# Forty of DOWN's 128 key blocks: both parts of the inputs in one matmul of 512 columns

## The chip, the cores and the metric

The kernel runs on one core of a Trainium2 chip. The metric is the device time of one execution in microseconds (us); the time before is the median of three runs. The engines are named as in the profile: PE is TensorE (PEld its weight loads), DVE is VectorE, ACT is ScalarE, POOL is GpSimd, and SP issues the DMAs of the weights.

## The reference

Two transformer blocks work one after the other on 256 tokens of width 1024, in float32. The change lies in the feed-forward layer of the first block, which picks experts by product keys. Cut to what matters:

```
qh = (xb @ w_pq).reshape(T, 8, 2, 128)                    # 8 heads, two half queries
s1, s2 = qh[:, :, 0] @ sub_keys1.T, qh[:, :, 1] @ sub_keys2.T
v1, i1 = top_k(s1, 16);  v2, i2 = top_k(s2, 16)           # routing, on VectorE here
cand_s = v1[..., :, None] + v2[..., None, :]              # 16 x 16 candidates
top_s, pos = top_k(cand_s, 16);  g = softmax(top_s)
a   = gelu(einsum(expert_down[eidx], xb))                 # DOWN
out = einsum(g * a, expert_up[eidx])                      # UP
```

The kernel gathers no experts. DOWN computes the products of all 16384 experts with all 256 tokens, takes the Gelu of them, and multiplies by a gate that is zero for experts that were not picked; UP sums over all experts.

## The kernel before

The expert matrix of DOWN is cut into 128 key blocks of 128 experts. Block j is one chunk `down{j}` of 128 x 1024 floats, that is eight weight tiles of 128 x 128. To be precise enough, each float32 operand is cut into a high and a low part: the chunk into `hi` and `lo`, the inputs into `XD[:, 0]` and `XD[:, 1]`. `unit_T` (line 343) makes three products for each of the eight tiles in `mm3` (lines 339 to 341): `hi` times the high inputs, `hi` times the low inputs, `lo` times the high inputs. All 24 matmuls of a block have 256 columns (the tokens) and add into one half of one PSUM bank; there are five such banks, tagged `mm`.

A chunk comes by DMA into `raw` (SP), is rounded into `hi` by ACT (line 123), and `lo = raw - hi` is made by POOL or by DVE (line 135). The table `PLAN` says which: POOL for blocks 0 to 20, DVE for 21 to 30, POOL for 31 to 47, and DVE from block 48 on. `Stream.take` runs ahead: when block j is taken, the program writes `hi` of block j+3 and `lo` of block j+2 into the engines' queues.

Each engine works through its own queue in the order in which the program wrote it. Behind the matmuls of block j, `ch.evac` first writes what reads the bank, `ev_down` (line 978; in DOWN's first blocks one Gelu on ACT from the bank to `cb[:, j]`, line 981), and then lets every running side chain take one step (`Chains.tick`). The side chain of importance here is `routing` (line 878). For each half of the tokens it takes 8 steps in which DVE searches the 16 best keys of two half heads (`top16`, lines 872 to 876, on 128 values), then 8 steps with the candidates of one head each (a sum in line 888 and `top16` on 256 values), then a softmax (lines 892 to 896, its exponential on ACT in line 893). Two ticks later PE transposes the result (line 899), and the gathering of the expert numbers follows (lines 902 to 926), with one more transpose on PE for each of the two key numbers (line 925). One step is written behind each block: the steps of the first 128 tokens behind blocks 0 to 15, their softmax behind block 16, the transpose behind block 18; for the second 128 tokens behind blocks 28 to 43, 44 and 46. When the routing is done the chain `gating` starts, which fills `cb` with gates while DOWN goes on.

Of the kernel before, what the change touches and what calls it, by code (L numbers as in the profile page):

```python
# [24 lines left out]
AF = mybir.ActivationFunctionType  # L25
OP = mybir.AluOpType
# [26 lines left out]
for _name, _w in (("avg", 3), ("aq", 4), ("mk", 2), ("mq", 2), ("mv", 4), ("mo", 4), ("xk", 8), ("xv", 8),  # L53
# [18 lines left out]
          ("keys", 0): 1, ("keys", 1): 1, ("keys", 2): 3, ("keys", 3): 1, ("keys", 4): 2, ("queries", 1): 3,  # L72
          ("gla", 1): 1, ("gla", 8): 1, ("gla_out", 2): 1}

PLAN = {"mv0": ("AV",), "xo2": ("AG",), "down21": ("AV",), "down31": ("AG",), "down48": ("AV",),
        "upw0": ("AV", "AG"), "upw122": ("AV",), "up3": ("AV", "AG"), "up31": ("AV",)}

# [72 lines left out]
class Chains:  # L150
# [23 lines left out]
    def evac(self, name, fns):  # L174

        self.held.append((name, fns))
        self.flush()
        self.tick()
# [30 lines left out]
def block_kernel(ctx, tc, xT, memT, pT, wst, dwn, upw, keysT, gate_w2, cols, rows, out):  # L209
    nc = tc.nc  # L210
    V, A, G, T = nc.vector, nc.scalar, nc.gpsimd, nc.tensor
# [17 lines left out]
    ws = Stream(nc, rawp, splitp, order, 3, 4)  # L229

    ws.plan = PLAN
    ch = Chains()
# [40 lines left out]
    def bank(pool, tag, **kw):  # L273
        return pool.tile([128, 512], FT, tag=tag, name=tag, bufs={"mm": 5, "at": 3}[tag], **kw)
# [63 lines left out]
    def mm3(ps, wh, wl, xh, xl, start, stop):  # L338
        T.matmul(ps, lhsT=wh, rhs=xh, start=start, stop=False)  # L339
        T.matmul(ps, lhsT=wh, rhs=xl, start=False, stop=False)  # L340
        T.matmul(ps, lhsT=wl, rhs=xh, start=False, stop=stop)  # L341

    def unit_T(pool, name, xs, evac, ks=range(8), needs=()):

        for c in needs:
            ch.finish(c)
        wh, wl = ws.take(name)
        ps = bank(pool, "mm")[:, :256]
        for i, kd in enumerate(ks):
            mm3(ps, wh[:, kd * 128:kd * 128 + 128], wl[:, kd * 128:kd * 128 + 128], xs[0][:, kd], xs[1][:, kd],  # L350
                i == 0, i == 7)
        ch.evac(name, [lambda: evac(ps)])

    def pair_T(pool, units, xs, at=6):
# [46 lines left out]
    with ExitStack() as es:  # L401
# [305 lines left out]
        def unit_first(name, i):  # L707
            key = f"{name}{i}"
            if name == "mv":
                unit_N(psA, [f"mv{k}" for k in range(4)], xs,  # L710
                       lambda tb, ps: A.activation(v1[:, tb, :, 0:128], ps.rearrange("p (h d) -> p h d", h=4), AF.Copy,
                                                   scale=rx[:, tb:tb + 1]))
            elif name == "mo":
                unit_N(psA, [f"mo{k}" for k in range(4)], xs, ev_mo)
            elif name == "avg":
                unit_N(psA, ["avg0", "avg1", "avg2"], xs, ev_avg, n=264)
            elif name == "aq":
                unit_T(psA, key, xs, times(aqT[:, i]))
            elif name in ("mk", "mq"):
                unit_T(psA, key, xs, lambda ps: ev_conv(ps, i + 2 * (name == "mk")))  # L720
            else:
                unit_T(psA, key, (memh, meml), split_times(kxh[:, i], kxl[:, i], Rm, G), needs=("mem",))
# [5 lines left out]
        for n in range(8):  # L728
            unit_T(psA, f"wo{n}", (mixh, mixl), add_and_prep(n, "g_cross", wk), ks=(4, 5, 6, 7, 0, 1, 2, 3),
                   needs=("window", "mlstm"))  # L730
# [65 lines left out]
    with ExitStack() as es:  # L796
        big = es.enter_context(tc.tile_pool(name="big", bufs=1))
        psD = psB = ctx.enter_context(tc.tile_pool(name="psD", bufs=4, space=PSUM))
        XD = big.tile([128, 2, 8, 256], FR)
        cb = big.tile([128, 128, 256], FT)  # L800
# [4 lines left out]
        J0 = 80  # L805
# [124 lines left out]
        front = {"j": 0, "t": 0}  # L930
# [16 lines left out]
        def gating():  # L947
# [10 lines left out]
            for t4 in range(64):  # L958
# [16 lines left out]
                    make(t4 // 2 * 8 + 8, t4 % 2)  # L975
                yield 1

        def ev_down(ps, j):
            t = front["t"]
            if t < 256:  # L980
                A.activation(cb[:, j, t:256], ps[:, t:256], AF.Gelu)
            if t > 0:
                A.activation(ps[:, 0:t], ps[:, 0:t], AF.Gelu)
                V.tensor_tensor(cb[:, j, 0:t], ps[:, 0:t], cb[:, j, 0:t], op=OP.mult)
            front["j"] = j + 1
# [7 lines left out]
        def coef(j):  # L993

            if j % 4 == 0:
                ring[0] = xp.tile([128, 4, 2, 256], FR, tag=("XH", "XL")[j // 4 % 2], name="ring")
            hi, lo = ring[0][:, j % 4, 0], ring[0][:, j % 4, 1]
            A.activation(hi, cb[:, j], AF.Copy, scale=1.0 / GATE)  # L998
            V.scalar_tensor_tensor(lo, cb[:, j], 1.0 / GATE, hi, op0=OP.mult, op1=OP.subtract)  # L999
            coefs[j] = hi, lo  # L1000

        for j in range(128):
            if j == 127:

                ch.finish("gating")
                coef(0)
                coef(1)
            unit_T(psD, f"down{j}", (XD[:, 0], XD[:, 1]), lambda ps, j=j: ev_down(ps, j), needs=("routing",) if j == J0 else ())

        sums = [[bank(psB, "mm") for tb in range(2)] for g in range(2)]  # L1010
        nat2 = flat[:, 4096:6144].rearrange("p (a d) -> p a d", a=2)
# [75 lines left out]
    with ExitStack() as es:  # L1087
# [409 lines left out]
        for n in range(8):  # L1497
            ps = bank(psA, "mm")[:, 0:256]
            for q4 in range(4):
                wh, wl = ws.take(f"dn{n * 4 + q4}")  # L1500
# [10 lines left out]
        for c in range(2):  # L1511
            wh, wl = ws.take(f"ple{c}")
            for i in range(4):
                ps = bank(psA, "mm")[:, 0:256]
# [123 lines left out]
```

## Time and profile before

| | us |
|---|---|
| median of 3 runs | 1550.6 (1550.4 to 1552.74) |
| the profiled execution, its own time | 1549.96 |
| its span, first to last instruction | 1548.3 |
| DOWN, first matmul | 283.6 |
| last matmul of DOWN | 686 |
| routing on VectorE, first 128 tokens | 282.9 to 335.7 |
| routing on VectorE, second 128 tokens | 367.7 to 418.7 |

The rows that the prediction reads stand in the section before it. All times of rows are microseconds from the start of the span. In a timeline a row has its start, its duration, the engine, the line, the operation and what it works on; matmuls overlap, so the pace of PE is read from the starts, not from the durations. On DVE and ACT too an instruction can start a little before the one ahead of it has ended, so what an instruction takes of its engine is read from start to start.

### The profile page before, as it was taken

How to read it: one execution, taken by the hardware profiler on the slowest of the kernel's cores; microseconds unless marked ns; L12 is line 12 of the kernel's file. 1: busy time of each engine (PE TensorE's matmuls, PEld its weight loads, DVE VectorE, ACT ScalarE, POOL GpSimd, SP SyncE). 2: the span in 40 equal slices, each digit the busy share in tenths (PEclk: the TensorE clock that was granted, in tenths of full speed). 3: DMA queues.
4: the chain of work that ended last, by engine and by line, in shares of the span. 5: the costliest groups of instructions: out<-in, count | busy, mean ns of one | idle time of the engine just before them, and what ended most of it. 6: DMA issues, size and time to landing. Idle time of an engine off the chain costs nothing.

```text
span 1548.3 us, 27502 instructions
## 1 busy us (share of the span) xinstructions
PE 1524.9 (98%) x10818; PEld 1417.4 (92%) x10818; DVE 1137.9 (73%) x2037; ACT 805.9 (52%) x1370; POOL 428.4 (28%) x239
## 2 busy tenths in 40 slices
PE   9899999999999999999999999998999999999998
PEld 8799999999999999998888888887888999999998
DVE  7977754877978899967777777768984656876456
ACT  7665553554545555454555445546754644544443
POOL 2220067654600000024444444403130000386000
PEclk9899999999999999999999999999999999999999
DMA  8335455456555554465666666655564465566553
GB/s 271 118 110 166 140 162 175 142 165 200 172 178 155 152 160 153 153 190 196 196 191 191 193 195 196 193 161 169 150 194 133 124 190 164 170 192 215 180 183 117
DMA packets 75713, 265.32 MB, mean 171 GB/s; under 512 B 8368, under 2 KB 11952, under 8 KB 75584
## 3 DMA queue, kind: packets, MB, share of 16 engines
q1 hardware_dynamic: 74848, 262.31, 54.0%
q8 instruction: 84, 1.38, 0.4%
q10 hardware_dynamic: 736, 1.27, 0.2%
q14 instruction: 45, 0.37, 0.1%
HBM read 262.49 MB, written 1.05 MB: 170 GB/s over the span
## 4 chain that ended last, share of the span: by engine, by line
PE 90%; DVE 6%; DMA 1%; ACT 1%; issue 1%; POOL 0%; SPq 0%; ACTq 0%; DVEq 0%; POOLq 0%
PE mm L339 18%; PE mm L341 18%; PE mm L340 18%; PE mm L1017 8%; PE mm L1018 8%; PE mm L1019 7%; PE mm L379 3%; PE mm L380 3%; PE mm L378 3%; PE at L964 2%; DVE lo L135 1%; DVE nww L298 1%; DMA rowt<-in_rows 0%; DMA memt<-in_memT 0%; DVE m L686 0%
## 5 line engine op out<-in xcount | busy, mean ns | idle before, releaser
L123 ACT CAST hi<-raw 128x1024 fp32r<-128x1024 f32 (+1 forms) x495 | 516.8, 1046 | 281.1 <-issue 169.0
L135 POOL TENSOR_TENSOR lo<-raw,hi 128x1024 fp32r<-128x1024 f32 x135 | 326.7, 2421 | 725.3 <-ACT hi L123 723.2
L135 DVE TENSOR_TENSOR lo<-raw,hi 128x1024 fp32r<-128x1024 f32 (+1 forms) x360 | 444.1, 1243 | 22.3 <-ACT hi L123 21.7
L339 PE MATMUL mm<-XD,hi 128*128 128x256 f32 x1024 | 295.6, 289 | 0.0
L340 PE MATMUL mm<-XD,hi 128*128 128x256 f32 x1024 | 289.7, 283 | 0.0
L341 PE MATMUL mm<-XD,lo 128*128 128x256 f32 x1024 | 289.5, 283 | 0.0
L999 DVE SCALAR_TENSOR_TENSOR ring<-cb,ring 128x256 fp32r<-128x256 f32 x128 | 172.6, 1350 | 92.5 <-ACT ring L998 92.5
L1017 PE MATMUL mm<-hi,ring 128*128 128x512 f32 x512 | 199.3, 389 | 0.0
L1018 PE MATMUL mm<-lo,ring 128*128 128x512 f32 x512 | 199.2, 389 | 0.0
L1019 PE MATMUL mm<-hi,ring 128*128 128x512 f32 x512 | 199.2, 389 | 0.0
L340 PEld LDWEIGHTS mm<-XD,hi 128*128 128x128 f32 x1024 | 196.2, 192 | 0.0
L341 PEld LDWEIGHTS mm<-XD,lo 128*128 128x128 f32 x1024 | 196.0, 191 | 0.0
L339 PEld LDWEIGHTS mm<-XD,hi 128*128 128x128 f32 x1024 | 196.0, 191 | 0.0
L339 PE MATMUL mm<-XH,hi 128*128 128x256 f32 x584 | 168.5, 289 | 1.5 <-DVE cb L390 0.9
L341 PE MATMUL mm<-XH,lo 128*128 128x256 f32 x584 | 165.9, 284 | 0.6 <-DVE lo L135 0.6
L340 PE MATMUL mm<-XL,hi 128*128 128x256 f32 x584 | 165.9, 284 | 0.0
L339 PEld LDWEIGHTS mm<-XH,hi 128*128 128x128 f32 x584 | 112.6, 193 | 3.1 <-issue 1.5
L1019 PEld LDWEIGHTS mm<-hi,ring 128*128 128x128 f32 x512 | 96.1, 188 | 20.1
L1017 PEld LDWEIGHTS mm<-hi,ring 128*128 128x128 f32 x512 | 96.1, 188 | 19.9
L1018 PEld LDWEIGHTS mm<-lo,ring 128*128 128x128 f32 x512 | 96.1, 188 | 19.7
L341 PEld LDWEIGHTS mm<-XH,lo 128*128 128x128 f32 x584 | 112.7, 193 | 0.8 <-DVE lo L135 0.8
L340 PEld LDWEIGHTS mm<-XL,hi 128*128 128x128 f32 x584 | 112.6, 193 | 0.2
(468 smaller groups left out, 2966.8 us busy)
## 6 DMA issues: line engine op xcount, KB each, us to landing
raw<-in_wst SPq DMA_DIRECT2D x237, 512.0 KB, 3.8
raw<-in_dwn SPq DMA_DIRECT2D x128, 512.0 KB, 3.7
raw<-in_upw SPq DMA_DIRECT2D x128, 512.0 KB, 3.9
hT<-in_xT SPq DMA_DIRECT2D x4, 256.0 KB, 4.7
memt<-in_memT SPq DMA_DIRECT2D x1, 1024.0 KB, 6.2
out<-hT SPq DMA_DIRECT2D x7, 128.0 KB, 1.7
rowt<-in_rows ACTq DMA_DIRECT2D x1, 640.0 KB, 6.7
raw<-in_wst SPq DMA_DIRECT2D x2, 256.0 KB, 3.6
```

Of the source, the lines that this page charges most:

```text
L123: self.nc.scalar.copy(hi[:, o], raw[:, o])
L135: (self.nc.vector if eng == "V" else self.nc.gpsimd).tensor_tensor(lo[:, o], raw[:, o], hi[:, o], op=OP.subtract)
L339: T.matmul(ps, lhsT=wh, rhs=xh, start=start, stop=False)
L340: T.matmul(ps, lhsT=wh, rhs=xl, start=False, stop=False)
L341: T.matmul(ps, lhsT=wl, rhs=xh, start=False, stop=stop)
L378: T.matmul(pss[tb], lhsT=xh, rhs=h, start=kd == 0, stop=False)
L379: T.matmul(pss[tb], lhsT=xh, rhs=l, start=False, stop=False)
L380: T.matmul(pss[tb], lhsT=xl, rhs=h, start=False, stop=kd == 7)
L999: V.scalar_tensor_tensor(lo, cb[:, j], 1.0 / GATE, hi, op0=OP.mult, op1=OP.subtract)
L1017: T.matmul(o, lhsT=ch, rhs=wh, start=j == 0, stop=False)
L1018: T.matmul(o, lhsT=ch, rhs=wl, start=False, stop=False)
L1019: T.matmul(o, lhsT=cl, rhs=wh, start=False, stop=j == 127)
```

## The change

For blocks 0 to 39 the block is computed by a new function, `unit_W`. It uses the whole bank: `hi` meets both parts of the inputs side by side in one matmul of 512 columns (the high inputs' sums in columns 0 to 255, the low inputs' in 256 to 511), and `lo` meets the high inputs in a matmul of 256 columns that adds into columns 0 to 255. That makes 16 matmuls in place of 24, with as many columns in all. The two sums of the bank are added on the way out by `ev_wide`: ACT copies columns 256 to 511 into `cb[:, j]`, DVE adds columns 0 to 255 to it, and ACT takes the Gelu of `cb[:, j]` in place. The Gelu of block j is written only with the evacuation of block j+1 (`settle`). Blocks 40 to 127 are as before.

```diff
+WIDE = 40
...
+    def unit_W(pool, name, x2, evac, needs=()):
...
+        for kd in range(8):
+            wide = lambda: T.matmul(ps, lhsT=wh[:, kd * 128:kd * 128 + 128], rhs=x2[:, :, kd], start=kd == 0,
+                                    stop=kd == 7)
+            if kd < 7:
+                wide()
+            T.matmul(ps[:, 0:256], lhsT=wl[:, kd * 128:kd * 128 + 128], rhs=x2[:, 0, kd], start=False, stop=False)
+            if kd == 7:
+                wide()
         ch.evac(name, [lambda: evac(ps)])
...
+        def settle():
+
+            if "open" in front:
+                j = front.pop("open")
+                A.activation(cb[:, j], cb[:, j], AF.Gelu)
+                front["j"] = j + 1
+
+        def ev_wide(ps, j):
+            assert front["t"] == 0
+            settle()
+            A.copy(cb[:, j], ps[:, 256:512])
+            V.tensor_tensor(cb[:, j], ps[:, 0:256], cb[:, j], op=OP.add)
+            front["open"] = j
+
         def ev_down(ps, j):
+            settle()
...
-            unit_T(psD, f"down{j}", (XD[:, 0], XD[:, 1]), lambda ps, j=j: ev_down(ps, j), needs=("routing",) if j == J0 else ())
+            needs = ("routing",) if j == J0 else ()
+            if j < WIDE:
+                unit_W(psD, f"down{j}", XD, lambda ps, j=j: ev_wide(ps, j), needs)
+            else:
+                unit_T(psD, f"down{j}", (XD[:, 0], XD[:, 1]), lambda ps, j=j: ev_down(ps, j), needs=needs)
```

Lines of the changed kernel are some 20 higher than those of the kernel before: 891 to 895 are the old 872 to 876 (`top16`), 907 is the old 888, 911 to 915 the old 892 to 896, 137 and 125 the old 135 and 123.

**VectorE at the start of DOWN.** Before, behind the last tile of `XD` only searches of the routing follow (`cb` is also the storage of the routing's tables):

```order
L866 TENSOR_TENSOR XD<-cb,XD 128x256 [waits Activation_49] x2
L872 MAX cb<-cb 128x8
L873 MAX_INDEX cb<-cb 128x8 [waits DVE_49]
L874 MATCH_REPLACE cb<-cb 128x128
L875 MAX cb<-cb 128x8 [waits DVE_49]
L876 MAX_INDEX cb<-cb 128x8 [waits DVE_49]
L872 MAX cb<-cb 128x8
```

With the change:

```order
L885 TENSOR_TENSOR XD<-cb,XD 128x256 [waits Activation_49] x2
L1008 TENSOR_TENSOR cb<-mm,cb 128x256 [waits Activation_49]
L891 MAX cb<-cb 128x8
L892 MAX_INDEX cb<-cb 128x8 [waits DVE_49]
L893 MATCH_REPLACE cb<-cb 128x128
L894 MAX cb<-cb 128x8 [waits DVE_49]
L895 MAX_INDEX cb<-cb 128x8 [waits DVE_49]
L891 MAX cb<-cb 128x8
```

The add of block 0 (line 1008) now stands ahead of the routing's first step, and the add of each further block up to 39 stands ahead of the step of that block.

**ScalarE at the same place.** Before, casts of the weights (`hi`) and Gelus from the bank (`mm`) take turns, and each Gelu waits only for PE:

```order
L123 CAST hi<-raw 128x1024 [waits DMAHW7_49,Pool_49]
L981 ACT_TABLE_LOAD
L981 ACTIVATE cb<-mm 128x256 [waits PE_49]
L123 CAST hi<-raw 128x1024 [waits DMAHW0_49,Pool_49]
L981 ACTIVATE cb<-mm 128x256 [waits PE_49]
L123 CAST hi<-raw 128x1024 [waits DMAHW1_49,Pool_49]
```

With the change:

```order
L125 CAST hi<-raw 128x1024 [waits DMAHW7_49,Pool_49]
L1007 COPY cb<-mm 128x256 [waits PE_49]
L125 CAST hi<-raw 128x1024 [waits DMAHW0_49,Pool_49]
L1001 ACT_TABLE_LOAD
L1001 ACTIVATE cb<-cb 128x256 [waits DVE_49]
L1007 COPY cb<-mm 128x256 [waits PE_49]
L125 CAST hi<-raw 128x1024 [waits DMAHW1_49,Pool_49]
L1001 ACTIVATE cb<-cb 128x256 [waits DVE_49]
L1007 COPY cb<-mm 128x256 [waits PE_49]
L125 CAST hi<-raw 128x1024 [waits DMAHW2_49,Pool_49]
```

Each Gelu now waits for DVE (its block's add), and the copy of the next block and the cast of a later chunk stand behind it.

**VectorE around the softmax of the first 128 tokens.** Before, the softmax, the reading of the transpose (`gT`), and the first steps of the gathering up to the first `lo` that DVE makes, that of block 21:

```order
L892 TENSOR_TENSOR cb<-cb 128x128
L894 TENSOR_REDUCE cb<-cb 128x8 [waits Activation_49]
L895 RECIPROCAL cb<-cb 128x8 [waits DVE_49]
L896 TENSOR_TENSOR cb<-cb 128x128 [waits DVE_49]
L902 TENSOR_SCALAR gT<-at 128x128 [waits PE_49]
L903 SCALAR_TENSOR_TENSOR gT<-at,gT 128x128 [waits DVE_49]
L907 TENSOR_SCALAR cb<-cb 128x128
L910 CAST cb<-cb 128x128 [waits DVE_49]
L912 CAST cb<-cb 128x256
L914 TENSOR_TENSOR cb<-cb,iota_96 128x2048 [waits DVE_49]
L135 TENSOR_TENSOR lo<-raw,hi 128x1024 [waits DMAHW1_49,Activation_49]
```

With the change:

```order
L911 TENSOR_TENSOR cb<-cb 128x128
L913 TENSOR_REDUCE cb<-cb 128x8 [waits Activation_49]
L914 RECIPROCAL cb<-cb 128x8 [waits DVE_49]
L915 TENSOR_TENSOR cb<-cb 128x128 [waits DVE_49]
L1008 TENSOR_TENSOR cb<-mm,cb 128x256 [waits Activation_49] x2
L921 TENSOR_SCALAR gT<-at 128x128 [waits PE_49]
L922 SCALAR_TENSOR_TENSOR gT<-at,gT 128x128 [waits DVE_49]
L926 TENSOR_SCALAR cb<-cb 128x128
L929 CAST cb<-cb 128x128 [waits DVE_49]
L931 CAST cb<-cb 128x256
L933 TENSOR_TENSOR cb<-cb,iota_96 128x2048 [waits DVE_49]
L137 TENSOR_TENSOR lo<-raw,hi 128x1024 [waits DMAHW1_49,Pool_49]
```

Between the softmax and the reading of the transpose stand the adds of blocks 17 and 18, which wait for copies on ACT; behind the shown rows come the add of block 19, the rest of the step and `lo` of block 22.

## Rows read from the trace of the kernel before

**Rows 1.** The page: busy time of each engine over the whole span, and the chain of work that ended last, by engine.

```profile
PE 1524.9 (98%) x10818; PEld 1417.4 (92%) x10818; DVE 1137.9 (73%) x2037; ACT 805.9 (52%) x1370; POOL 428.4 (28%) x239
...
PE 90%; DVE 6%; DMA 1%; ACT 1%; issue 1%; POOL 0%; SPq 0%; ACTq 0%; DVEq 0%; POOLq 0%
```

**Rows 2.** Busy time by stretch, four stretches of ten microseconds in which DOWN and the routing run together (start and end, length, busy time and number of instructions for each engine, granted clock as a share of 2.4 GHz, DMA share, GB/s).

```profile
core 0: us, PE busy (x) PEld busy (x) DVE busy (x) ACT busy (x) POOL busy (x), PEclk, DMA share, GB/s
...
300.00:310.00 10.00, 10.00 (x85) 10.00 (x85) 9.38 (x48) 4.20 (x7) 8.58 (x4) 1.00 0.61 183
...
320.00:330.00 10.00, 10.00 (x86) 10.00 (x85) 9.52 (x33) 4.05 (x7) 8.58 (x4) 1.00 0.61 179
380.00:390.00 10.00, 10.00 (x86) 10.00 (x85) 9.35 (x52) 4.47 (x7) 8.09 (x5) 1.00 0.54 168
400.00:410.00 10.00, 10.00 (x86) 10.00 (x85) 9.52 (x32) 4.64 (x7) 8.10 (x5) 1.00 0.56 178
```

**Rows 3.** Timeline of TensorE in DOWN (start in us, duration in us, engine, line, operation): a matmul of 256 columns, and the 24th one after it.

```profile
300.07 0.28 PE L341 MATMUL mm<-XD,lo 128*128 128x256 f32 x1
...
302.95 0.28 PE L341 MATMUL mm<-XD,lo 128*128 128x256 f32 x1
```

**Rows 4.** Timeline of TensorE in UP: a matmul of 512 columns, and the twelfth one after it.

```profile
850.12 0.39 PE L1019 MATMUL mm<-hi,ring 128*128 128x512 f32 x1
...
852.84 0.39 PE L1019 MATMUL mm<-hi,ring 128*128 128x512 f32 x1
```

**Rows 5.** Timeline of VectorE over the routing of the first 128 tokens: the first search of a first and of a second step (two half heads each), then the sums that open the first, the second and the last of the eight candidate steps, then the first subtraction of the softmax.

```profile
282.87 0.29 DVE L872 MAX8 cb<-cb 128x8 f32<-128x128 f32 x1
...
286.02 0.27 DVE L872 MAX8 cb<-cb 128x8 f32<-128x128 f32 x1
...
307.99 0.41 DVE L888 TENSOR_TENSOR cb<-cb 128x256 f32<-128x256 f32 x1
...
310.69 0.41 DVE L888 TENSOR_TENSOR cb<-cb 128x256 f32<-128x256 f32 x1
...
327.64 0.60 DVE L888 TENSOR_TENSOR cb<-cb 128x256 f32<-128x256 f32 x1
...
330.53 0.45 DVE L892 TENSOR_TENSOR cb<-cb 128x128 f32<-128x128 f32 x1
```

**Rows 6.** Timeline of VectorE just ahead of DOWN: a product of a PSUM bank with a tile, and the instruction behind it.

```profile
275.97 0.42 DVE L390 TENSOR_TENSOR cb<-mm,Rb 128x256 f32<-128x256 f32 x1 [2.46 <-PE mm L341]
276.31 0.89 DVE L862 SCALAR_TENSOR_TENSOR cb<-hT,colt,Rb 128x256 f32<-128x256 f32 x2
```

**Rows 7.** Timelines of ScalarE and of GpSimd in DOWN: the Gelu of a block, the cast behind it, and the subtraction on GpSimd that this cast lets start.

```profile
289.59 0.38 ACT L981 ACTIVATE cb<-mm 128x256 f32<-128x256 f32 x1 [1.56 <-PE mm L341]
289.87 1.04 ACT L123 CAST hi<-raw 128x1024 fp32r<-128x1024 f32 x1
...
290.98 2.43 POOL L135 TENSOR_TENSOR lo<-raw,hi 128x1024 fp32r<-128x1024 f32 x1 [0.47 <-ACT hi L123]
```

**Rows 8.** Timelines of TensorE, ScalarE and VectorE: DOWN's first matmul, then the softmax of the first 128 tokens and the transpose on TensorE that reads its last result (in brackets the idle time ahead, and who ended it).

```profile
283.56 0.36 PE L339 MATMUL mm<-XD,hi 128*128 128x256 f32 x1
...
334.48 0.31 ACT L893 ACTIVATE cb<-cb 128x128 f32<-128x128 f32 x1
...
334.83 0.29 DVE L894 TENSOR_REDUCE cb<-cb 128x8 f32<-128x128 f32 x1 [3.85 <-ACT cb L893]
...
335.39 0.29 DVE L896 TENSOR_TENSOR cb<-cb 128x128 f32<-128x128 f32 x1
...
338.35 0.27 PE L899 MATMUL at<-ident,cb 128*128 128x128 f32 x1
...
338.66 0.29 DVE L902 TENSOR_SCALAR gT<-at 128x128 f16<-128x128 f32 x1 [2.98 <-PE at L899]
```

**Rows 9.** Timelines behind that transpose: the cast and the table load on ScalarE, the subtractions of blocks 21 and 22 on VectorE, and the first matmul of block 21 on TensorE.

```profile
334.70 1.03 ACT L123 CAST hi<-raw 128x1024 fp32r<-128x1024 f32 x1
335.75 1.28 ACT L981 ACT_TABLE_LOAD   x1
...
340.92 1.22 DVE L135 TENSOR_TENSOR lo<-raw,hi 128x1024 fp32r<-128x1024 f32 x1
...
345.03 1.22 DVE L135 TENSOR_TENSOR lo<-raw,hi 128x1024 fp32r<-128x1024 f32 x1
...
344.22 0.28 PE L339 MATMUL mm<-XD,hi 128*128 128x256 f32 x1
```

**Rows 10.** Timelines over the routing of the second 128 tokens: the cast on VectorE that stands ahead of its first search, the last product of its softmax, the last matmul of block 46 and the transpose behind it.

```profile
367.68 0.29 DVE L926 CAST eT<-at 128x128 f16<-128x128 f32 x1 [3.29 <-PE at L925]
...
418.45 0.29 DVE L896 TENSOR_TENSOR cb<-cb 128x128 f32<-128x128 f32 x1
...
419.20 0.28 PE L341 MATMUL mm<-XD,lo 128*128 128x256 f32 x1
419.32 0.27 PE L899 MATMUL at<-ident,cb 128*128 128x128 f32 x1
```

**Rows 11.** Timelines of GpSimd and VectorE at one candidate sum, and the group of all 16 candidate sums (count, busy us, mean ns).

```profile
392.12 2.40 POOL L135 TENSOR_TENSOR lo<-raw,hi 128x1024 fp32r<-128x1024 f32 x1 [0.48 <-ACT hi L123]
...
393.02 1.78 DVE L888 TENSOR_TENSOR cb<-cb 128x256 f32<-128x256 f32 x1
...
L888 DVE TENSOR_TENSOR cb<-cb 128x256 f32<-128x256 f32 x16 | 10.1, 632 | 0.0
```

More of the change, by code (lines that the diff above doesn't have):

```diff
@@ L351, in unit_T @@
                 i == 0, i == 7)
+        ch.evac(name, [lambda: evac(ps)])
+    def unit_W(pool, name, x2, evac, needs=()):
+        for c in needs:
+            ch.finish(c)
+        wh, wl = ws.take(name)
+        ps = bank(pool, "mm")
+        for kd in range(8):
[6 more added lines that the diff above has]
+                wide()
         ch.evac(name, [lambda: evac(ps)])
```

## The prediction

> **What bounds the kernel now.** I read the page's busy times and the chain first: PE is busy for 98% of the span and makes 90% of the chain [rows 1]. That says that shorter PE work pays, but DVE's 73% is a mean over stages, so next I read the stretches in which DOWN and the routing overlap. There PE is busy without a gap at the granted clock 1.00, that is 2.4 GHz, ACT is half idle, and DVE is busy 9.35 to 9.52 of 10 us [rows 2]. The reader is to see that DVE is as full as PE there, and that this costs nothing today, because no matmul of blocks 0 to 20 waits for DVE: the banks are emptied by ACT, and POOL makes `lo`. Third, I read where PE and DVE meet. PE's transpose behind block 18 came 2.67 us after DVE's last softmax product had ended (335.68 against 338.35), and DVE then waited for PE [rows 8]. Behind block 46 the product ended at 418.74 and PE came at 419.32 [rows 10]: 0.58 us of room.
>
> **What PE saves.** 24 matmuls of 256 columns take 2.88 us [rows 3], 120 ns each. Twelve of 512 columns take 2.72 us [rows 4], 226.7 ns each. The columns stay the same and eight starts fall away: 8 x 226.7 + 8 x 120 = 2774 ns, which is 106 ns less than 2880. Over 40 blocks that is **4.25 us**, all of it on the path. No row shows a moving operand in two pieces 8 KB apart; bounds are 226.7 ns (UP's, one piece) and 240 ns (two of 256), the latter saving nothing. I take 226.7, since the columns of each piece lie together as UP's do.
>
> The Trainium skill (TensorE: Matmul & The Clock Gate, Back-to-back issue gap) puts a matmul's gap at its columns at 2.4 GHz plus some 2.5 ns, so eight starts would be 20 ns and 40 blocks 0.8 us. Here the fixed part is 120 - 106.7 = 13 ns in rows 3 and the same in rows 4, so the rows decide; by the page the forecast below would be 3.4 us later.
>
> **What DVE and ACT get.** DVE gets one add per block. Its nearest row, a product of a bank with a tile, lasts 0.42 us and the next instruction starts 0.34 later [rows 6]; I take 0.34, with 0.42 as the other end. ACT has a copy (0.28 from start to start, as the Gelu from a bank in rows 7) and a Gelu from SBUF (I take 0.3) in place of one Gelu: 0.3 us more per block of 2.77 on a half idle engine, hidden unless ACT is held. But it is held: in the new order each Gelu waits for DVE's add, and the next copy and the cast of a later chunk queue behind it. That cast (1.04) and POOL's `lo` (2.43) [rows 7] feed a block four further on, so some 6 us of lateness on DVE pass unseen, and more holds PE.
>
> **First hold-up, the softmax of the first 128 tokens.** A step of two half heads takes 286.02 - 282.87 = 3.15 us, the eight candidate steps with what precedes the softmax take 330.53 - 307.99 = 22.5 [rows 5]. With the add a step costs 3.49 and about 3.15 against PE's 2.774 per block, so DVE falls back at every block. Also, the routing now starts at 282.87, before DOWN's first matmul; then the add of block 0 stands ahead of it: 283.56 [rows 8] + 2.77 + 0.1 (drain) + 0.38 (copy) + 0.05 + 0.34 = 287.2, or 4.3 later. Sixteen more adds lie ahead of the softmax: 5.4. It starts at 330.53 + 4.3 + 5.4 = 340.2. Its wait of 3.85 for ACT disappears [rows 8], since ACT has by then done its copy; 0.45 + 0.31 (the exponential) + 0.85 (334.83 to 335.68) and hand-overs of 0.1 end it at 341.9. PE without a wait is through block 18 at 283.56 + 19 x 2.774 = 336.3. PE loses **5.6 us**, part of it already at blocks 14 to 18 by way of ACT's queue; the sum is the same.
>
> **Second, the change to DVE's `lo` at block 21.** Behind the exponential ACT has a cast (1.05 to the next start), a table load (1.29) [rows 9], the Gelu of 16, the copy of 17, a cast, the Gelu of 17 and the copy of 18 (0.3 + 0.28 + 0.94 + 0.3 + 0.38): 4.5 us. Only then can DVE add block 18, and in its queue the reading of the transpose stands behind that add: 4.9 us behind the exponential where PE's transpose would be ready at 1.25. So `lo` of block 21 comes 3.7 us later against PE. Today it ends at 342.14, 2.1 before the block's first matmul at 344.22 [rows 9], with the shorter blocks 1.9: 1.8 lost. `lo` of block 22 ends at 346.25 today, 0.85 ahead of that block (344.22 + 2.88); late by 3.7 and one more add, it costs another 1.7. The ends are 0 and 3.5; I take **3.0**, since ACT may make up a part while PE stands.
>
> **Third, the softmax of the second 128 tokens.** Its first step starts behind block 28 [rows 10], with 0.6 us more for the copy and add of that block, and 11 adds (blocks 29 to 39) make 3.7. PE comes 11 x 0.106 = 1.2 earlier, and the room is 0.58: 0.6 + 3.7 + 1.2 - 0.6 = **4.9 us**.
>
> **Fourth, the candidate sums.** They take 0.41 us alone [rows 5], 0.63 in the mean, and 1.78 where POOL was at work: that one ended 0.28 after POOL's instruction (392.12 + 2.40 = 394.52) [rows 11]. So it waited for POOL. Twelve of them will meet POOL at other phases: none waiting gives back 12 x 0.22 = 2.6; each waiting 1.37 costs 16.4 less that, 13.8. If DVE's add lets ACT go (0.3 + 0.28 + 1.04 + 0.1), POOL's `lo` ends 4.1 after the add, while the next sum would come after 3.15: that makes a step 3.6, 0.45 more. I count four such, **1.6 us** with rounding down, nearer to the mean row than to 1.78.
>
> Sum: -4.25 + 5.6 + 3.0 + 4.9 + 1.6 = **+10.9 us**. Against the profiled execution (1549.96, span 1548.3 and 1.7 around it) that is 1560.9; the median of the runs is 0.64 higher: **1561.5 us**. Nothing later gives it back, since PE is busy to the end; the one-block-late Gelu is settled at block 40, long before the gating reads it.
>
> **The rivals.** *DVE keeps up* (the adds hide in gaps): 1550.6 - 4.25 = 1546.3. For it speak ACT's idle half and the five banks; against it rows 2 and the arithmetic of 3.49 against 2.774 in one queue. 0.07. *One hold-up only*: DVE is late at the first softmax (5.6), but `lo` of 21 and 22 and the second softmax keep their room, because candidate sums that meet POOL less give up to 2.6 back: 1550.6 - 4.25 + 5.6 = 1552 less up to 2.6, no change. 0.08. *POOL decides*: the sums wait half of 13.8 instead of 1.6, which adds 5.3: 1567; it decides from the point where DVE's step, not PE's block, sets POOL's pace, and then each step is longer than the last sum assumes. 0.13. The Trainium skill (SBUF — State Buffer, Who interferes with whom) says that a DVE instruction with two SBUF inputs and a GpSimd one that reads SBUF exclude each other for the whole instruction; rows 11 agree, and the same page frees the new add, which has one SBUF input. *The wide matmul is paced as two of 256*: nothing saved, 1565.8 at most, less where DVE sets the pace anyway; 0.04. The TensorE page's smaller saving would land between that and the forecast and has no chance apart from it, as rows 3 and 4 measure the fixed part. That the change doesn't take place I leave out: the program has the 16 matmuls.
>
> **How the numbers follow.** My forecast, three hold-ups that outweigh the saving, has 0.68: 1561.5, from 1554.3 (no loss at block 21, sums that give 2.6 back) to about 1565. The rival on the other side, DVE keeping up, is the one below 1547.5. With POOL deciding and 0.08 per add in place of nothing (28 x 0.08 = 2.2) the upper end is 1569. Range 1554 to 1569. A measurement of this kernel tells some 0.2%, 3.1 us, from no change. Faster 0.07, same 0.08, slower 0.85.
>
> **What would show it.** The wide matmuls' starts alternate 227 and 120 ns. In the stretch 284 to 330 DVE has no idle time and each add comes later behind its block, up to some 8 us; ACT's Gelus wait for DVE. PE stands at the transpose behind block 18 and at the one behind block 46, several us each, with DVE's softmax product as the releaser, and at blocks 21 and 22 for `lo`. Blocks 23 to 39 run at 2.774. If PE has no wait at these places, the step that counted DVE's queue was wrong; if only the amounts differ, the meeting with POOL was.

## The result and the profile after

The changed kernel takes 1568.86 us (median of 4 runs, 1566.77 to 1570.41) against 1550.57 us before in the same job: the ratio is 1.0114, 95% interval 1.0101 to 1.0128. It is slower by 18.3 us, where 10.9 was forecast: the forecast is 7.4 us short, and the time lies 0.14 us below the upper end of its range. The profiled execution took 1570.41 us, its span 1568.5 us.

The page of the changed kernel, busy times and chain, answers to [rows 1]: PE has 320 matmuls fewer and 6 us more of busy time, and DVE's share of the chain rose from 6% to 14%.

```profile
PE 1530.6 (98%) x10498; PEld 1405.5 (90%) x10498; DVE 1156.0 (74%) x2077; ACT 818.8 (52%) x1410; POOL 428.1 (27%) x239
...
PE 82%; DVE 14%; ACT 1%; DMA 1%; issue 1%; POOL 0%; SPq 0%; ACTq 0%; DVEq 0%; POOLq 0%
```

DOWN, from its first to its last matmul, went from 402.76 us (283.56 to 686.32) to 419.85 us (286.14 to 705.99): 17.1 us of the difference lie there, where the change is. DOWN also starts 2.6 us later, in code that the change does not touch; the last two experiments below are about that.

**The saving.** TensorE's timeline in DOWN, answering to [rows 3]: a wide matmul and, sixteen starts on, the same one of the next block.

```profile
300.68 0.40 PE L364 MATMUL mm<-XD,hi 128*128 128x512 f32 x1
300.91 0.28 PE L368 MATMUL mm<-XD,lo 128*128 128x256 f32 x1
301.03 0.40 PE L364 MATMUL mm<-XD,hi 128*128 128x512 f32 x1
...
303.50 0.39 PE L364 MATMUL mm<-XD,hi 128*128 128x512 f32 x1
```

The starts alternate 0.23 and 0.12 us, and a block takes 303.50 - 300.68 = 2.82 us, not 2.774. With 120 ns for the narrow one, a wide matmul takes 2820 / 8 - 120 = 233 ns, between the bounds of 226.7 and 240, and 40 blocks save 2.4 us, not 4.25.

**DVE falls back.** VectorE's timeline: the add of block 0 and the first search, the add of block 8 with the first candidate sum behind it, a later sum, and the softmax.

```profile
289.65 0.42 DVE L1008 TENSOR_TENSOR cb<-mm,cb 128x256 f32<-128x256 f32 x1 [4.13 <-ACT cb L1007]
290.00 0.28 DVE L891 MAX8 cb<-cb 128x8 f32<-128x128 f32 x1
...
317.44 0.40 DVE L1008 TENSOR_TENSOR cb<-mm,cb 128x256 f32<-128x256 f32 x1
317.77 1.03 DVE L907 TENSOR_TENSOR cb<-cb 128x256 f32<-128x256 f32 x1
...
339.10 1.01 DVE L907 TENSOR_TENSOR cb<-cb 128x256 f32<-128x256 f32 x1
...
346.20 0.28 DVE L911 TENSOR_TENSOR cb<-cb 128x128 f32<-128x128 f32 x1
...
347.41 0.29 DVE L915 TENSOR_TENSOR cb<-cb 128x128 f32<-128x128 f32 x1
```

A step of two half heads takes (317.44 - 289.65) / 8 = 3.47 us with its add; 3.49 was forecast, from the 3.15 of [rows 5]. A candidate step takes (346.20 - 317.77) / 8 = 3.55 us; 3.15 was forecast. The row of GpSimd's timeline and the group of all candidate sums on VectorE (count, busy us, mean ns) answer to [rows 11]:

```profile
337.44 2.39 POOL L137 TENSOR_TENSOR lo<-raw,hi 128x1024 fp32r<-128x1024 f32 x1 [1.23 <-ACT hi L125]
```

```profile
L907 DVE TENSOR_TENSOR cb<-cb 128x256 f32<-128x256 f32 x16 | 16.1, 1008 | 0.0
```

The sum at 339.10 ended at 340.11, 0.28 behind POOL's instruction (339.83), and the mean sum takes 1008 ns in place of 632.

**PE stands.** TensorE's waits between 284 and 455 us (line, released by, us in total, times, longest). Before there is none in this stretch.

```profile
PE at L918 <- ACT hi L125: 11.0, 2, 5.8
PE mm L368 <- POOL lo L137: 1.7, 4, 0.6
PE mm L368 <- DVE lo L137: 0.9, 1, 0.9
PE mm L343 <- POOL lo L137: 0.7, 2, 0.5
```

The first row is the two transposes behind blocks 18 and 46. The profile names ACT's cast as their releaser. That cast ended at 347.76 (its row is below), DVE's last product at 347.41 + 0.29 = 347.70, and the weight load of the transpose began at 347.82. It was DVE's product that counted: in four traces PE waits at both transposes (this one, and those of the way out alone, of the stands filled and of POOL still, below), and in all eight waits the weight load begins 0.115 or 0.116 us behind the end of DVE's product, but anything from 0.059 to 0.065 behind the end of the cast. The cast ends just there because it too stood behind the exponential, which waited for DVE. The chain runs from add to search to sum on DVE without a break from 290 to 346.2. Timelines of ScalarE and TensorE there, the cast and the table load answering to [rows 9], the transpose to [rows 8]:

```profile
346.51 0.31 ACT L912 ACTIVATE cb<-cb 128x128 f32<-128x128 f32 x1 [1.70 <-DVE cb L911]
346.73 1.03 ACT L125 CAST hi<-raw 128x1024 fp32r<-128x1024 f32 x1
347.77 1.28 ACT L1001 ACT_TABLE_LOAD   x1
...
342.31 0.40 PE L364 MATMUL mm<-XD,hi 128*128 128x512 f32 x1
347.85 0.45 PE L918 MATMUL at<-ident,cb 128*128 128x128 f32 x1 [5.14 <-ACT hi L125]
```

**And then the clock falls.** Busy time by stretch around the two stands, in the columns of [rows 2]:

```profile
340.00:345.00 5.00, 2.71 (x15) 2.13 (x15) 4.76 (x17) 2.80 (x4) 2.38 (x1) 1.00 0.49 120
345.00:352.00 7.00, 4.15 (x14) 3.60 (x15) 3.31 (x12) 5.46 (x9) 2.37 (x1) 0.51 0.29 80
352.00:356.00 4.00, 4.00 (x24) 3.50 (x24) 3.97 (x8) 2.37 (x6) 0.00 (x0) 1.00 0.27 108
429.00:434.00 5.00, 2.77 (x24) 2.56 (x22) 4.76 (x17) 0.00 (x0) 1.53 (x1) 0.99 0.67 206
434.00:440.70 6.70, 3.11 (x15) 3.14 (x16) 6.00 (x19) 4.42 (x7) 0.00 (x0) 0.50 0.14 27
440.70:445.00 4.30, 4.30 (x38) 4.30 (x38) 4.16 (x7) 1.96 (x3) 0.00 (x0) 1.00 0.52 201
```

The reader is to see the column before the last but one: 1.00, then 0.51 and 0.50 (that is 1.2 GHz), then 1.00 again. In both places PE had stood and came back to work at the lower level. No stretch of DOWN in the kernel before shows that.

**The sum of DOWN**, from the starts of the blocks in TensorE's timelines, each against the same block before, less 0.06 us up to block 39:

| | forecast | measured |
|---|---|---|
| 40 shorter blocks | -4.25 | -2.4 |
| blocks 15 to 18, short waits and the first stand | 5.6 | 8.1 |
| block 19 at the lower clock | none | 1.8 |
| wait for `lo` of blocks 21 and 22 (measured: of 22 alone) | 3.0 | 1.1 |
| blocks 43, 44, 46, short waits and the second stand | 4.9 | 7.2 |
| block 47 at the lower clock | none | 1.3 |
| candidate sums | 1.6 | in the hold-ups |
| sum | 10.9 | 17.1 |

### The profile page after: what moved, and what is told of

The parts are those of the page before. It is cut to its first block, busy times and chain, and to the rows that moved or that the text cites. A ratio compares the mean times of both kernels' runs of the same rounds, so it can differ in the third digit from the quotient of the medians.

```text
span 1568.5 us, 26977 instructions
## 1 busy us (share of the span) xinstructions
PE 1530.6 (98%) x10498; PEld 1405.5 (90%) x10498; DVE 1156.0 (74%) x2077; ACT 818.8 (52%) x1410; POOL 428.1 (27%) x239
## 4 chain that ended last, share of the span: by engine, by line
PE 82%; DVE 14%; ACT 1%; DMA 1%; issue 1%; POOL 0%; SPq 0%; ACTq 0%; DVEq 0%; POOLq 0%
PE mm L341 15%; PE mm L343 15%; PE mm L342 15%; PE mm L1057 7%; PE mm L1055 7%; PE mm L1056 7%; PE mm L399 3%; PE mm L398 3%; PE mm L397 3%; PE at L983 2%; DVE lo L137 1%; DVE cb L895 1%; DVE cb L892 1%; DVE cb L894 1%; DVE cb L893 1%
## 5 line engine op out<-in xcount | busy, mean ns | idle before, releaser
L341 PE MATMUL mm<-XD,hi 128*128 128x256 f32 x704 | 205.4, 292 | 0.0
L343 PE MATMUL mm<-XD,lo 128*128 128x256 f32 x704 | 199.7, 284 | 0.7 <-POOL lo L137 0.7
L342 PE MATMUL mm<-XD,hi 128*128 128x256 f32 x704 | 199.7, 284 | 0.0
L343 PEld LDWEIGHTS mm<-XD,lo 128*128 128x128 f32 x704 | 135.5, 192 | 1.1 <-POOL lo L137 1.1
L342 PEld LDWEIGHTS mm<-XD,hi 128*128 128x128 f32 x704 | 135.8, 193 | 0.0
L341 PEld LDWEIGHTS mm<-XD,hi 128*128 128x128 f32 x704 | 135.6, 193 | 0.0
```

## The experiments

Theory Q: what is lost comes from DVE's queue, by the added adds and by the sums that meet POOL, and the lower clock follows from PE's stands. Rival M: the wide matmuls themselves make it. The first four kernels below were timed beside before at 1550.03 us; the one with the quiet blocks, the two with the inputs side by side and the one with the later transposes beside 1550.38; the others beside 1550.26. Lengths of DOWN are from first to last matmul, 402.76 before and 419.85 after.

**The way out alone.** Blocks 0 to 39 by narrow matmuls, with the changed way out:

```diff
-                unit_W(psD, f"down{j}", XD, lambda ps, j=j: ev_wide(ps, j), needs)
+                unit_T(psD, f"down{j}", (XD[:, 0], XD[:, 1]), lambda ps, j=j: ev_wide(ps, j), needs=needs)
...
-            A.copy(cb[:, j], ps[:, 256:512])
-            V.tensor_tensor(cb[:, j], ps[:, 0:256], cb[:, j], op=OP.add)
+            A.copy(cb[:, j], ps[:, 0:256])
+            V.tensor_tensor(cb[:, j], ps[:, 0:256], cb[:, j], op=OP.max)
```

> Blocks 0 to 39 are computed as in the kernel before (24 matmuls of 256 columns), but leave their bank in the changed way: a copy on ACT, an operation of the add's size on DVE (the larger of the copy and the bank, which are equal), the Gelu one block later. Theory Q (DVE's queue carries the loss): PE stands at the transposes behind blocks 18 and 46 as in the changed kernel, the granted clock falls to 0.50 behind each stand, and the time is 1569 to 1571 us: the 0.06 us that a wide block saves is lost too, but for the blocks whose lateness is hidden by the stands. Rival M (the wide matmuls themselves make the loss): no stand, 1550 to 1551 us.

Measured: 1568.63 us, ratio 1.0122 (1.0105 to 1.0139), DOWN 420.32 us. Its waits of TensorE in the same stretch:

```profile
PE at L918 <- ACT hi L125: 10.9, 2, 5.8
PE mm L343 <- POOL lo L137: 1.3, 4, 0.5
PE mm L343 <- DVE lo L137: 0.7, 1, 0.7
```

The stands are those of the changed kernel, with not one wide matmul in the program. Rival M falls. The time is 0.4 us below what was expected. The 2.4 us of the wide matmuls are worth only 420.32 - 419.85 = 0.5 us beside them: a PE that reaches the transpose earlier stands there longer.

**Without the add.**

```diff
-            A.copy(cb[:, j], ps[:, 256:512])
-            V.tensor_tensor(cb[:, j], ps[:, 0:256], cb[:, j], op=OP.add)
+            A.copy(cb[:, j], ps[:, 0:256])
```

> Wide matmuls in blocks 0 to 39, but DVE's add is left out: ACT copies columns 0 to 255 and takes the Gelu one block later, so the products of the low inputs are missing from the result. Theory Q: no stand at the transposes, clock 1.00 through all of DOWN, blocks of 2.82 us in place of 2.88, so 1550.6 - 40 x 0.06 = 1548.2 us. Rival A (ACT's doubled work and its order hold the casts): stands remain, over 1555 us. Rival M (wide matmuls): about 1568 us.

Measured: 1548.99 us, ratio 0.9994 (0.9984 to 1.0004), DOWN 400.20 us, 2.56 less than before. Busy time where the changed kernel stood:

```profile
340.00:345.00 5.00, 5.00 (x30) 4.39 (x29) 4.90 (x9) 3.56 (x8) 0.00 (x0) 1.00 0.48 121
345.00:352.00 7.00, 7.00 (x42) 6.11 (x41) 5.86 (x8) 4.08 (x8) 0.00 (x0) 1.00 0.59 216
```

PE is busy without a gap, at 2.4 GHz. The copy and the second Gelu on ACT are hidden. The whole difference of 419.85 - 400.20 = 19.65 us hangs on one DVE instruction per block, 0.33 us from its start to the next (317.44 to 317.77 above): on its own time, 40 x 0.33 = 13 us of DVE, and on ACT's wait for it, which goes with it here. An add that ACT doesn't wait for was not run; the run with POOL still, below, shows what the meeting of the sums with POOL is worth of it.

**The stands filled.** Forty matmuls that nobody needs, ahead of each of the two transposes:

```diff
-                ps = bank(psD, "at")[:, 0:128]
+                ps = bank(psD, "at")
+                for _ in range(40):
+                    T.matmul(ps[:, 0:256], lhsT=XD[:, 0, 0, 0:128], rhs=XD[:, 0, 0], start=True, stop=True)
+                ps = ps[:, 0:128]
                 T.transpose(ps, ee, ident)
```

> The changed kernel with 40 additional matmuls of 256 columns (4.8 us at 0.12) ahead of each of the two transposes that read a softmax, so that PE works through most of the time in which it stood; their result is not used. Theory Q with the clock: the granted clock stays 1.00 behind blocks 18 and 46, blocks 19 and 47 take 2.82 and 2.88 us in place of 4.72 and 4.28, and the time falls by 1.9 + 1.4 = 3.3 us to 1565.6 us though 80 matmuls were added. Rival (the clock falls there for another reason than PE's stand): both drops remain and the time is 1569 us or more.

Measured: 1565.95 us (1565.32 to 1566.88), ratio 1.0104 (1.0088 to 1.0121), DOWN 418.45 us. The same stretches:

```profile
345.00:352.00 7.00, 6.62 (x46) 5.98 (x46) 3.30 (x12) 5.26 (x10) 2.40 (x1) 1.00 0.20 73
352.00:356.00 4.00, 2.80 (x16) 2.14 (x15) 3.93 (x10) 2.26 (x5) 0.00 (x0) 1.00 0.35 123
...
434.00:440.70 6.70, 5.70 (x48) 5.52 (x48) 6.00 (x19) 4.14 (x7) 0.00 (x0) 1.00 0.10 18
```

Of its waits of TensorE between 284 and 455 us:

```profile
PE mm L368 <- DVE lo L137: 2.6, 2, 1.4
```

The clock stays at 1.00 in all of them: it had fallen because PE stood. But of the 3.3 us only 1.4 came back in DOWN, those of block 47 (the other 1.5 us by which the median fell lie outside DOWN, where nothing was changed). Behind the first stand the full clock brought PE sooner to blocks 21 and 22, and there it lost 4.26 + 4.45 - 2 x 2.82 = 3.1 us (lengths of the two blocks) to waits for `lo`, in place of 1.1. So the lower clock cost nothing of its own at the first stand; it lay on a wait that was there anyway. The time came out near the 1565.6 us expected, but not by that sum.

**POOL still during the sums.**

```diff
+NO_LO = {f"down{j}" for j in (*range(8, 21), *range(36, 48))}
...
             raw = self.raws.pop(c)
+            if self.order[c][0] in NO_LO:
+                self.parts[c] = (hi, hi)
+                self.second += 1
+                continue
```

> The changed kernel, but POOL makes no lo for blocks 8 to 20 and 36 to 47: their matmuls read hi twice, so the product with the low weights is wrong there. POOL is idle while DVE makes the candidate sums. Theory Q with the meeting of the sums and POOL as one of its terms: each sum takes 0.41 us in place of 1.01, DVE ends each softmax some 4.8 us earlier, the hold-ups of 8.2 and 7.2 us shrink to about 3.4 and 2.4, and the time is 1555 to 1559 us (the lower end if the clock no longer falls). Rival (the sums' waits lie in time in which DVE would have been idle): 1566 to 1569 us.

Measured: 1558.78 us, ratio 1.0055 (1.0038 to 1.0071), DOWN 409.89 us. The group of the candidate sums:

```profile
L912 DVE TENSOR_TENSOR cb<-cb 128x256 f32<-128x256 f32 x16 | 6.6, 414 | 0.0
```

DOWN is 9.96 us shorter than in the changed kernel, half of the 19.65. A sum takes 414 ns in place of 1008, 9.5 us less for sixteen, and the hold-ups shrink from 8.1 to 3.9 and from 7.2 to 1.9 us: together 9.5. From its first search DVE reaches the first softmax 4.2 us sooner, and its eight sums up to there are 4.2 us shorter. The Trainium skill (SBUF — State Buffer, Who interferes with whom) says that a DVE instruction with two SBUF inputs, which this sum is, and a GpSimd instruction that reads SBUF exclude each other; the 1008 and the 414 ns agree. The time is at the upper end of what was expected, since behind the first hold-up the clock fell again (block 19 took 5.27 us).

**Wide blocks only where DVE does not search.**

```diff
-WIDE = 40
+WIDE = {*range(17, 28), *range(47, 57)}
...
-            if j < WIDE:
+            if j in WIDE:
```

> Wide matmuls only in blocks 17 to 27 and 47 to 56, between the stretches in which DVE searches; the way out of these blocks is the changed one. Theory Q: DVE has room there, no stand over 1 us, clock 1.00 through DOWN, and 21 blocks save 0.06 us each: DOWN takes 401.6 us in place of 402.9, the time is about 1549 us, not to be told from before. Rival (the way out costs wherever it stands, by the order on ACT): stands at the transposes behind blocks 18 and 46 again, above 1555 us.

Measured: 1550.16 us, ratio 1.0004 (0.9995 to 1.0014), DOWN 402.94 us. No stand, as expected, but no gain either. TensorE's waits from 284 to 470 us, of which before has none:

```profile
PE mm L368 <- DVE lo L137: 0.6, 2, 0.4
PE at L983 <- DVE hots L964: 0.5, 1, 0.5
```

PE now waits for DVE's `lo` of blocks 22 and 27 and for the first operand of the gating behind block 57. These three blocks are longer by 0.4, 0.6 and 0.6 us, a little more than the wide matmuls save. That it is the 21 adds that make DVE late there is argued, not shown by a run of its own.

**High and low inputs side by side in memory**, once without the add and once in the quiet blocks:

```diff
-        XD = big.tile([128, 2, 8, 256], FR)
+        XK = big.tile([128, 8, 2, 256], FR)
+        XD = XK.rearrange("p n a t -> p a n t")
...
-            wide = lambda: T.matmul(ps, lhsT=wh[:, kd * 128:kd * 128 + 128], rhs=x2[:, :, kd], start=kd == 0,
+            wide = lambda: T.matmul(ps, lhsT=wh[:, kd * 128:kd * 128 + 128], rhs=x2[:, kd], start=kd == 0,
```

> As the run without DVE's add (wide matmuls in blocks 0 to 39, the products of the low inputs left out of the result), but XD lies in memory so that the high and the low inputs of one tile stand side by side: the 512 columns of a wide matmul are one piece in place of two pieces 8 KB apart. If the two pieces make the wide matmul 233 ns in place of UP's 227 ns, a block falls from 2.82 to 2.77 us and DOWN from 400.3 to 398.5 us. If something else does (a narrow matmul with another weight behind each wide one), the block stays at 2.82 us and DOWN at 400.3 us.

> Wide matmuls in blocks 17 to 27 and 47 to 56 alone, and the high and low inputs side by side in memory. If one piece makes the wide matmul as fast as UP's (227 ns): 21 x 0.106 = 2.2 us, DOWN 400.7 us, time about 1548 us, the best of all kernels here. If the layout makes no difference: as the run with the same blocks and the old layout, DOWN 401.6 us.

Measured: 1548.87 us, ratio 0.9993 (0.9983 to 1.0002), DOWN 400.28 us; and 1550.40 us, ratio 1.0001 (0.9992 to 1.0011), DOWN 402.63 us. With the two pieces apart DOWN took 400.20 and 402.94. In the quiet blocks DOWN is again 1 us longer than the 401.6 expected, by the same three waits. The pieces are not what makes a wide matmul 233 ns.

**All wide matmuls first**, without the add:

```diff
         for kd in range(8):
-            wide = lambda: T.matmul(ps, lhsT=wh[:, kd * 128:kd * 128 + 128], rhs=x2[:, :, kd], start=kd == 0, ...
+            T.matmul(ps, lhsT=wh[:, kd * 128:kd * 128 + 128], rhs=x2[:, :, kd], start=kd == 0, stop=False)
+        for kd in range(8):
+            T.matmul(ps[:, 0:256], lhsT=wl[:, kd * 128:kd * 128 + 128], rhs=x2[:, 0, kd], start=False, stop=kd == 7)
```

> As the run without DVE's add (the products of the low inputs are left out of the result), but each block does its eight wide matmuls first and its eight narrow ones behind them. If the taking of turns between wide and narrow makes a wide matmul 233 ns in place of UP's 227 ns, a block falls from 2.82 to 2.77 us and DOWN from 400.3 to 398.5 us. If the wide matmul itself takes 233 ns here, DOWN stays at 400.3 us.

Measured: 1549.43 us, ratio 0.9994 (0.9983 to 1.0004), DOWN 399.36 us, 0.84 less than with turns. TensorE's timeline, eight to a row, and the last three of the first eight by themselves:

```profile
300.92 2.00 PE L364 MATMUL mm<-XD,hi 128*128 128x512 f32 x8
302.76 1.12 PE L366 MATMUL mm<-XD,lo 128*128 128x256 f32 x8
303.71 2.00 PE L364 MATMUL mm<-XD,hi 128*128 128x512 f32 x8
```

```profile
302.08 0.84 PE L364 MATMUL mm<-XD,hi 128*128 128x512 f32 x3
```

Eight wide ones take 302.76 - 300.92 = 1.84 us, 230 ns each. Taking turns makes about half of the 6 ns above UP's 226.7; neither expectation held alone. The other half lies in the first five of the eight, which stand behind narrow ones: (302.08 - 300.92) / 5 = 232 ns each, while the last three take (302.76 - 302.08) / 3 = 227, as in UP. Why the first five take longer stays open.

**The transposes later**, by two blocks each:

```diff
-                yield 2
+                yield 4
                 ps = bank(psD, "at")[:, 0:128]
                 T.transpose(ps, ee, ident)
```

> The changed kernel with both transposes of a softmax written four ticks behind the softmax in place of two, so two blocks (5.6 us) later. Theory Q: DVE ends the softmax as late as now, but PE has two more blocks to compute meanwhile; the stands shrink from 5.3 and 5.9 us to under 1.5, the clock stays 1.00 in DOWN, what is left are the short waits of blocks 15 to 17, of 21 to 24 for lo and of 43 to 46, some 6 to 9 us in all: 1556 to 1560 us. Rival (PE stands for the search as such, wherever the transpose stands, since all queues run full): stands of over 4 us, 1565 us or more.

Measured: 1569.04 us, ratio 1.0122 (1.0105 to 1.0138), DOWN 420.24 us. My expectation fell. TensorE's waits from 284 to 455 us:

```profile
PE mm L343 <- DVE lo L137: 7.4, 1, 7.4
PE mm L368 <- POOL lo L137: 4.1, 6, 1.9
PE mm L364 <- ACT hi L125: 1.6, 1, 1.6
```

No transpose is in the list any more. PE stood at block 48 instead. POOL makes `lo` of blocks 31 to 47, DVE that of 48: its subtraction stood in DVE's queue behind the search. In the first half PE waited for `hi` and for POOL's `lo`, which ACT's held queue delayed.

**The transposes later, and `lo` of blocks 48 to 51 by POOL.**

```diff
-        ... "down48": ("AV",),
+        ... "down52": ("AV",),
```

> The run with the later transposes, and POOL in place of DVE makes lo of blocks 48 to 51, so that nothing that PE needs stands behind the second search on DVE but the transpose. Theory Q, as the run with the later transposes corrected it (the backlog shows wherever PE next takes something from DVE): PE's wait of 7.4 us at block 48 for lo disappears, PE comes to the transpose when the softmax is just done, the first hold-up stays as it is there (about 10 us at blocks 15 to 21), the time is 1559 to 1561 us. Rival (the backlog comes out at another place all the same, by ACT's held casts): 1565 us or more.

Measured: 1569.14 us, ratio 1.0118 (1.01 to 1.0136), DOWN 419.88 us. The rival was right. ScalarE's and TensorE's timelines at the second softmax:

```profile
429.84 1.28 ACT L912 ACT_TABLE_LOAD   x1
441.21 0.31 ACT L912 ACTIVATE cb<-cb 128x128 f32<-128x128 f32 x1 [10.09 <-DVE cb L911]
441.43 1.03 ACT L125 CAST hi<-raw 128x1024 fp32r<-128x1024 f32 x1
...
442.51 0.58 PE L341 MATMUL mm<-XD,hi 128*128 128x256 f32 x1 [4.47 <-ACT hi L125]
444.93 0.58 PE L343 MATMUL mm<-XD,lo 128*128 128x256 f32 x1 [1.63 <-POOL lo L137]
```

ACT stood 10.1 us at the exponential, which waits for DVE's search, and the casts of the next chunks stood behind it. Three ways lead from DVE's backlog to PE: the transpose, `lo`, and ACT's queue. With one or two of them closed DOWN is the same to 0.4 us. That is partly chance: TensorE's waits did shrink, from 14.3 us in all in the changed kernel to 13.3 and 12.0, but behind them the clock fell here too, against what was expected of the first of the two runs:

```profile
347.90:354.60 6.70, 4.90 (x16) 4.15 (x17) 3.50 (x5) 5.61 (x11) 1.74 (x1) 0.50 0.40 116
440.00:450.20 10.20, 6.07 (x26) 5.77 (x27) 4.20 (x8) 6.46 (x10) 4.74 (x2) 0.50 0.31 93
```

In this run PE worked for 4.90 + 6.07 = 11.0 us at the lower clock, in the one before it for 9.4 (350.3 to 357.0 and 439.0 to 445.7 us), in the changed kernel for 4.15 + 3.11 = 7.3. With half of these times as an estimate of what the clock cost, it took back about what the waits gave.

**The kernel before, twice more.**

> The kernel before once more, for its granted clock ahead of DOWN: if the fall at 243 us, which every profile of a changed kernel shows and the one of before does not, comes and goes from run to run, it can be seen here; if it belongs to the change, DOWN starts at 283.6 us again, with no fall.

> The kernel before a third time, with the same question as the run ahead of it: a fall of the granted clock at 243 us or none, DOWN's start at 284.7 to 287.3 or at 283.6 us.

Measured: 1549.89 and 1552.52 us; DOWN starts at 285.68 and 285.87, and takes 402.77 us in the first, as in the first profile. Busy time of the first by stretch:

```profile
238.00:245.00 7.00, 3.93 (x29) 3.54 (x29) 5.99 (x17) 2.24 (x3) 3.62 (x2) 0.97 0.70 216
245.00:248.00 3.00, 3.00 (x16) 3.00 (x16) 0.90 (x3) 0.06 (x1) 2.38 (x1) 0.50 0.04 15
```

And of the profile of before that the prediction read:

```profile
245.00:248.00 3.00, 3.00 (x27) 3.00 (x27) 0.70 (x2) 0.91 (x1) 1.92 (x1) 1.00 0.05 8
```

PE is idle for 3.05 to 3.07 us between 238 and 245, and at the lower clock behind it, in both runs; in the profile of before that the prediction read it is idle for as long, 7.00 - 3.93 = 3.07, and at 1.00 behind it. The profiles of the changed kernels have the fall too. So 2.1 to 2.3 of the 2.6 us by which DOWN started later are found without the change, and DOWN's length is the cleaner measure.

## Why the prediction came out as it did

- **DVE's queue as the bound: right.** The add taken away, the loss is gone; the add kept on narrow matmuls, the loss stays. The places were right: the transposes behind blocks 18 and 46, and `lo` of 22 (of 21 too once the stands were filled). The step of 3.49 us was 3.47; the first search was forecast 287.2 - 283.56 = 3.6 us behind DOWN's first matmul, and came 290.00 - 286.14 = 3.9 behind it.
- **The fourth term, the candidate sums: mis-sized.** "Nearer to the mean row than to 1.78" gave 1.6 us. They took 16 x (1.008 - 0.632) = 6.0 us more. The rival "POOL decides" put half of 13.8 there, 6.9, and was nearer on this term; its 1567 us, too. The runs showed in its place: DVE's step now sets the pace of ACT and so of POOL, and nearly every sum finds POOL at work (14 of the 16 take 0.86 us or more, two 0.41), since add, Gelu, copy, cast and `lo` follow from DVE's add in a fixed distance. I had seen that loop, but counted it for four steps alone.
- **Its part in the hold-ups.** 5.6 + 4.9 + 1.6 = 12.1 was forecast, 8.1 + 7.2 = 15.3 measured. The sums account for 4.4 more; PE, whose blocks are 0.046 us longer than forecast, came 0.9 and 0.5 later and took 1.4 of them back.
- **The saving: mis-sized.** 2.4 us for 4.25, as the wide matmul takes 233 ns in turns with narrow ones. UP's row had only wide ones.
- **`lo` of 21 and 22: right in size.** 3.0 was forecast. In the changed kernel 1.1 of it is wait, at block 22, and 1.8 was already lost to the lower clock at block 19; with the stands filled the wait is 3.1.
- **The clock: a term that the sum lacked.** No row of before showed a fall in DOWN, and I bounded none for a PE that stands. Net it is 1.3 us, those of block 47.
- **The range: partly luck.** Its upper end of 1569 was POOL deciding and 0.08 us more for every add. POOL did much as that rival said, but an add took 0.33 to 0.35 us from its start to the next, as in the forecast; what filled the rest was the smaller saving and the clock, which that end did not hold. The prediction's last sentence put any difference in the amounts down to the meeting with POOL; that is 4.4 us of it, the saving is 1.85 and the clock 1.3.
- Beyond DOWN, the median's 18.3 - 17.1 = 1.2 us are within what runs of either kernel differ by.

Added up from the forecast: 10.9 + 3.2 (hold-ups with sums) + 1.85 (saving) + 1.3 (clock) = 17.3, against 17.1 in DOWN.

## What to carry to other kernels

An instruction added to an engine that is 95% busy over a stretch can cost its time at every step there, short as it is (0.33 us in each block here), and what PE saves meanwhile mostly lengthens its wait (0.5 of 2.4 us was left). Before moving the place where PE meets such an engine, list every way from its queue to PE, those by a third engine's queue among them; giving slack at one or two of them gained 1 to 2 us of waits here, and the lower clock took them back. Where a queue falls back, ask also which shared resource it will now meet at every step, and whether the engine that is made to wait will come back at the lower clock.

## What was not expected of the hardware

- A matmul of 512 columns takes 233 ns in turns with one of 256, whether its columns are one piece or two 8 KB apart, and 226.7 in UP. In a row of eight behind narrow ones the first five take 232 and the last three 227. Why was not found.
- Behind the stands of PE in DOWN the granted clock was 0.50 to 0.51, and 1.00 when other matmuls filled the stands: 80 useless matmuls made the kernel no slower, in DOWN 1.4 us faster.
